# Hybrid layer with 32 experts: one set of 19 places for raw weights and their split parts, and a new order of experts

## The chip, the cores and the metric

The kernel runs on one core of one Trainium2 chip. The metric is the device time of one execution in microseconds; before the change it is 1484.7 us, the median of 3 runs (1482.25 to 1488.44).

## What is computed

512 tokens of 1024 numbers go through one layer: an input projection, four retention heads and eight sliding-window attention heads, an output projection `w_out` with a residual, then a mixture of 32 experts of which each token takes four, and last a gate with a small per-layer embedding and a final norm. The experts are nearly all of the weights:

```python
def expert_block(args):
    xblk, e = args
    h = xblk @ w_up[e] + b_up[e]
    return clamped_swiglu(h) @ w_down[e] + b_down[e]
```

`w_up[e]` is 1024 x 2048 and `w_down[e]` 1024 x 1024, both fp32: 12 MB for each expert.

## The kernel before

**Stages.** Stage 1 makes both kinds of heads, until about 227 us. The output projection, the router and the slot tables follow, until about 300 us; then the experts one after the other, until 1392 us; then the embedding gate and the norms.

**Pieces.** Weights arrive in pieces of 128 x 2048 fp32 (1 MB), eight for an expert's up products (`w_up_piece`) and four for its down products (`w_down_piece`). The list `pieces` holds their order: the four pieces of `w_out`, the eight up pieces of expert 0, and then for each expert the up pieces of the next one and the four down pieces of this one. `prefetch()` takes a place from the list `free`, issues the next piece's transfer on SP's queue (which works in order, a waiting transfer holds all behind it) and puts it on `queue`. Before the change `free` grows to 12 places, in three pools: three (`rawp`) from the start, five (`raw2`) once the memory of stage 1 is released, four (`raw3`) as the mixed heads are used up. At that release the kernel also makes `R.bias` from the down and up biases, on one of the raw places.

**Experts.** The string `BIG` says which experts get 128 rows ("L", 18 of 32) and which 64 ("S", 14). For an L expert each piece is split for three fp32r products: `split()` has ACT write `wh`, the rounded piece (L150), and DVE `wl`, what the rounding left out (L151). `wh` and `wl` have three rotating buffers each (`whp`, `wlp`). `up()` (L847) does for each up piece four products of `xTh` with `wh`, four of `xTl` with `wh`, four of `xTh` with `wl`; `down()` (L928) does for each down piece two groups of six in the same order, with two columns each. An S expert doesn't split its pieces; it uses each piece raw with pairs of products on 64 columns (L864, `up64` and `down64`). A piece is taken by `next_piece()` (split) or `whole_piece()` (raw); both put the raw place back on `free` and call `prefetch()`.

**Order of the work.** In the loop over e, `up` of expert e comes first, then its activation (`act`: `sg` on ACT, `a` on DVE), the transposes of the next expert's tokens (`prep`, L300, or `prep64`, L815), then `down` of expert e - 1 and the transposes of the activation (`act_t`). The tokens of expert e + 1 come by an indirect DMA (`xe`, L800), the results leave by another (`acc`, L942). In `w_out`'s section (L307 to L309 by `mm3`) PE takes three products per row block; the last transposes of `y` in stage 1 are on L598. The scores of the attention (L479) are products of 64 rows, of one or the other half.

Of the kernel before, what the change touches and what calls it, by code (L numbers as in the profile page):

```python
# [11 lines left out]
F32 = mybir.dt.float32  # L12
# [10 lines left out]
P = 128  # L23
# [13 lines left out]
RAW1, RAW2, RAW3 = 3, 5, 4  # L37
# [9 lines left out]
BIG = [c == "L" for c in "LL" + "SLSLSLSLSLSLSLL" + "SLSLSLSLSLSLLLS"]  # L47
# [48 lines left out]
def hymba_kernel(ctx, tc, x, p, positions, rel_bias_table, g_mix_norm, w_in, b_in, ret_norm_g,  # L96
# [27 lines left out]
    rawp = pool(ctx, "rawp", RAW1)  # L124
    whp = pool(ctx, "whp", 3)
    wlp = pool(ctx, "wlp", 3)
# [7 lines left out]
    R = SimpleNamespace(eid={})  # L134
    free = [rawp] * RAW1

    def raw_tile(dt=F32):
        pl_ = free.pop(0)
        return pl_.tile([P, 2048], dt, name="raw"), pl_

    def split(raw, parts=None, dst=None):
        if dst is None:
            wh = whp.tile([P, 2048], F32R, name="wh")
            wl = wlp.tile([P, 2048], F32R, name="wl")
        else:
            wh, wl = dst
# [51 lines left out]

    pieces = [w_ret(0, 0), w_ret(0, 4), w_kv, w_half(w_in, 0, 2048), w_half(w_in, 4, 2048)]
# [6 lines left out]
    for e in range(1, E + 1):  # L206
        if e < E:
            pieces += [w_up_piece(e, k) for k in range(8)]
        pieces += [w_down_piece(e - 1, f) for f in range(4)]
    n_moe = len(pieces)  # L210
# [6 lines left out]
    def prefetch(after=None):  # L217
        if free and state["next"] < min(len(pieces), state["limit"]):
            t, pl_ = raw_tile()
            if after is not None:  # L220
                nc.scalar.activation(t[:, 0:1], after[:, 0:1], AF.Copy)
            pieces[state["next"]](t)
            queue.append((t, pl_))
            state["next"] += 1

    def next_piece(parts=None, dst=None, more=True):
        t, pl_ = queue.pop(0)
        r = split(t, parts, dst)
        free.append(pl_)
# [3 lines left out]

    def whole_piece(use):

        t, pl_ = queue.pop(0)
        use(t)
        free.append(pl_)
# [88 lines left out]
    raw3 = pool(ctx, "raw3", RAW3)  # L327
    mix = [raw3.tile([P, 2048], F32R, name="raw").rearrange("p (a k t) -> a p k t", a=2, k=KD) for _ in range(NT)]
# [6 lines left out]
    p1 = px.enter_context(ExitStack())  # L335
    actp = pool(p1, "actp")
# [9 lines left out]
    prefetch()  # L346
    nc.sync.dma_start(out=xts[1], in_=x_v[:, 1, :])
    prefetch()
# [116 lines left out]
    def attention(nb):  # L465
# [8 lines left out]
        for gp in range(2):  # L474

            s_ps = [sps.tile([P, 512], F32, name="s_ps").rearrange("p (a b) -> p a b", a=2) for _ in range(2)]
            for g in range(2):
# [800 lines left out]
```

## Time and profile before

| | |
|---|---|
| median of 3 runs | 1484.7 us |
| the profiled execution's time | 1485.38 us |
| its span | 1483.6 us |
| PE busy | 1351.3 us (91%), 6090 instructions |
| DVE busy | 830.1 us (56%) |
| ACT busy | 677.7 us (46%) |
| moved by DMA | 462.47 MB, mean 312 GB/s |
| up and down pieces, from issue to landing | 17.4 and 17.9 us, median |

A row of the timeline gives the start in us, the length, the engine, the line, the operation and its output and inputs, the count, and in brackets the idle time of the engine before it and what ended it. PE's lengths are those of pipelined products, whose ends are modelled: their starts tell more. `SPq` is the issue of a transfer on SP's queue. PEclk is the granted clock of TensorE, 1.00 being full speed (2.4 GHz).

### The profile page before, as it was taken

Reading aid. Unit: us, or ns where it says so; the run is one execution under the profiler, and the core shown is the slowest. Engines: PE = TensorE matmul, PEld = TensorE weight load, DVE = VectorE, ACT = ScalarE, POOL = GpSimd, SP = SyncE. Lnnn points to the kernel's source line nnn. Section 1 sums busy time; section 2 is a strip of 40 time slices with the busy share of each in tenths; the row PEclk is TensorE's granted clock in tenths of the full one; section 3 lists DMA queues with packets and bytes.
Section 4 is the critical chain, followed back from the end, with each engine's and each line's share of the span. In section 5 each row is a group of like instructions: output and inputs, shape, how many; then the busy total and the mean of one; then the engine's idle time right before and its main releaser. Section 6 shows DMA issues by size and latency. Waiting matters only on the chain. (4 is left out here: it accounts for less than half of the span.)

```text
span 1483.6 us, 16861 instructions
## 1 busy us (share of the span) xinstructions
PE 1351.3 (91%) x6090; PEld 907.1 (61%) x6091; DVE 830.1 (56%) x1005; ACT 677.7 (46%) x750; POOL 224.4 (15%) x238
## 2 busy tenths in 40 slices
PE   5999999588999999999999999999999999999885
PEld 4777777466657474655647657465655647675564
DVE  6637774776547263544637647354553726683356
ACT  5333443455536253543626535343452625573443
POOL 2213241474100000000000000000100000000023
PEclk9999999788999999999999999999999999999998
DMA  9332046667899999999999999999999999987511
GB/s 272 118 109 58 29 142 254 237 254 280 318 402 396 403 405 396 406 399 393 392 396 408 393 388 387 375 403 396 386 394 399 395 387 400 391 328 283 183 72 43
DMA packets 110427, 462.47 MB, mean 312 GB/s; under 512 B 10830, under 2 KB 29180, under 8 KB 77568
## 3 DMA queue, kind: packets, MB, share of 16 engines
q1 hardware_dynamic: 99584, 436.24, 74.8%
q0 software_dynamic: 10320, 24.52, 6.5%
q8 instruction: 49, 0.80, 0.2%
q10 hardware_dynamic: 432, 0.57, 0.1%
q14 instruction: 42, 0.34, 0.1%
HBM read 447.26 MB, written 18.73 MB: 314 GB/s over the span
## 5 line engine op out<-in xcount | busy, mean ns | idle before, releaser
L151 DVE TENSOR_TENSOR wl<-raw,wh 128x2048 fp32r<-128x2048 f32 (+2 forms) x243 | 530.2, 2222 | 151.8 <-ACT wh L150 143.8
L150 ACT ACTIVATE wh<-raw 128x2048 fp32r<-128x2048 f32 (+2 forms) x243 | 442.9, 1858 | 110.2 <-PE up L847 52.2
L864 PE MATMUL up<-raw,xTh 128*64 128x512 f32 x896 | 195.3, 594 | 0.0
L896 DVE TENSOR_SCALAR a<-up 128x512 f32<-128x512 f32 x50 | 32.9, 687 | 267.8 <-ACT sg L895 267.8
L847 PE MATMUL up<-wh,xTh 128*128 128x512 f32 x576 | 162.8, 405 | 9.2 <-ACT wh L150 7.8
L895 ACT ACTIVATE sg<-up 128x512 f32<-128x512 f32 x50 | 27.9, 595 | 297.0 <-issue 158.5
L847 PE MATMUL up<-wl,xTh 128*128 128x512 f32 x576 | 160.9, 401 | 2.2 <-DVE wl L151 2.2
L847 PE MATMUL up<-wh,xTl 128*128 128x512 f32 x576 | 161.0, 401 | 1.4 <-DVE xTl L292 1.4
L864 PEld LDWEIGHTS up<-raw,xTh 128*64 128x64 f32 x896 | 63.1, 137 | 124.6 <-issue 120.0
L847 PEld LDWEIGHTS up<-wh,xTh 128*128 128x128 f32 x576 | 108.7, 191 | 40.5 <-ACT wh L150 13.1
L847 PEld LDWEIGHTS up<-wl,xTh 128*128 128x128 f32 x576 | 109.0, 191 | 32.8 <-DVE wl L151 7.0
L847 PEld LDWEIGHTS up<-wh,xTl 128*128 128x128 f32 x576 | 109.8, 191 | 28.2 <-DVE xTl L292 1.8
L928 PE MATMUL dn<-wh,aTh 128*128 128x512 f32 x288 | 100.8, 434 | 23.8 <-ACT wh L150 23.8
L928 PE MATMUL dn<-wl,aTh 128*128 128x512 f32 x288 | 104.0, 446 | 15.9 <-DVE wl L151 15.9
L942 POOL DMA_INDIRECT acc<-y,slot_i x30 | 45.4, 1514 | 443.3 <-ACT y L937 434.8
L800 POOL DMA_INDIRECT xe<-xg,slot_i x30 | 31.9, 1064 | 485.9 <-PE dn L857 261.0
L864 PE MATMUL dn<-raw,aT 128*64 128x512 f32 x448 | 102.9, 598 | 0.0
L928 PE MATMUL dn<-wh,aTl 128*128 128x512 f32 x288 | 98.2, 425 | 0.0
L928 PEld LDWEIGHTS dn<-wh,aTh 128*128 128x128 f32 x288 | 59.4, 211 | 42.8 <-ACT wh L150 27.3
L928 PEld LDWEIGHTS dn<-wl,aTh 128*128 128x128 f32 x288 | 58.5, 212 | 35.5 <-DVE wl L151 23.1
L914 DVE SCALAR_TENSOR_TENSOR aTl<-tp,aTh 128x512 fp32r<-128x512 f32 x36 | 24.1, 689 | 90.2 <-ACT aTh L913 90.2
L928 PEld LDWEIGHTS dn<-wh,aTl 128*128 128x128 f32 x288 | 59.3, 206 | 15.0
(340 smaller groups left out, 1571.9 us busy)
## 6 DMA issues: line engine op xcount, KB each, us to landing
raw<-in_w_up_dram SPq DMA_DIRECT2D x256, 1024.0 KB, 17.4
raw<-in_w_down_dram SPq DMA_DIRECT2D x128, 1024.0 KB, 17.9
raw<-in_w_in_dram SPq DMA_DIRECT2D x32, 256.0 KB, 4.8
raw<-in_w_out_dram SPq DMA_DIRECT2D x4, 1024.0 KB, 5.0
raw<-in_w_ple_gate_dram SPq DMA_DIRECT2D x4, 1024.0 KB, 10.4
raw<-in_w_in_dram SPq DMA_DIRECT2D x3, 1024.0 KB, 5.7
xt<-in_x_dram SPq DMA_DIRECT2D x4, 512.0 KB, 6.5
h<-in_x_dram POOLq DMA_DIRECT2D x4, 512.0 KB, 7.6
```

The source lines that it names most:

```text
L150: R.split_act = nc.scalar.activation(to(wh), src(raw), AF.Copy)
L151: R.split_dve = nc.vector.tensor_tensor(out=to(wl), in0=src(raw), in1=to(wh).bitcast(F32), op=ALU.subtract)
L800: return nc.gpsimd.indirect_dma_start(out=dst[0:n, 0:D // h], out_offset=None, in_=xg.rearrange("s (h d) -> (s h) d", h=h), in_offset=bass ...
L847: nc.tensor.matmul(h[n // 2][:, n % 2 * 512:n % 2 * 512 + 512], lhsT=a[:, k, :], rhs=w[:, n * 512:(n + 1) * 512], start=(k == 0 and a is x ...
L864: R.pair = nc.tensor.matmul(o[v * 64:v * 64 + 64, c:c + 512], lhsT=xT[:, k, :], rhs=w[:, v * n + c:v * n + c + 512], start=False, stop=las ...
L895: nc.scalar.activation(sg[:, cs], hv[:, :, 0], AF.Silu, scale=ALPHA)
L896: nc.vector.tensor_scalar(a[:, cs], hv[:, :, 1], LIMIT + 1.0, 1.0 - LIMIT, op0=ALU.min, op1=ALU.max)
L914: nc.vector.scalar_tensor_tensor(flat(l[:, g4, :]), in0=flat(t), scalar=1.0 / ALPHA, in1=flat(h[:, g4, :]).bitcast(F32), op0=ALU.mult, op1 ...
L928: m = nc.tensor.matmul(o[:, n * 512:(n + 1) * 512], lhsT=a[:, k, :], rhs=w[:, kk * 1024 + n * 512:kk * 1024 + (n + 1) * 512], start=False, ...
L942: nc.gpsimd.indirect_dma_start(out=acc.rearrange("s (h d) -> (s h) d", h=h), out_offset=bass.IndirectOffsetOnAxis(ap=idx[0:n, :], axis=0), ...
```

## The change

All raw pieces now have named places, 19 in the end: a0 to a2 from the start, b0 to b8 in place of the five of `raw2`, c0 to c3 of the mixed heads, h0 to h2, which were `whp`. The pool `wlp` lives in stage 1 only. Afterwards `split()` takes two places for `wh` and `wl` by `raw_tile(part=True)`; a second list `spare` holds places that parts have given back: parts take from `spare` first and raw pieces from `free` first, each from the other list if its own is empty. `used()`, called behind a piece's products, appends its two places to `spare`. `room()` tells `prefetch()` whether to hold back: among the next `depth` pieces to be used it counts those that will be split (the others are in `plain`) and wants two places for each, less the places that earlier ones give back.

Besides: the last 15 experts come in a new order, with as many L and S; `xn` of the router lies on two raw places; `sg` is half as wide, `y` has one buffer; for e = 1 the turn of the next expert's tokens (`turn()`) comes behind the down products of expert 0; the score products are pinned in alternation of the two halves; all four `w_out` pieces come in the new `prefetch()`, which loops by itself; the gains of the end lie in the place of the tile `last`.

The core of the diff:

```diff
@@ -34,7 +34,7 @@
 LIMIT = 7.0
 S_MAX = float(ALPHA * LIMIT / (1.0 + math.exp(-ALPHA * LIMIT)))
 CAP = 96
-RAW1, RAW2, RAW3 = 3, 5, 4
+RAW1, RAW2, RAW3 = 3, 9, 4
 FAR = 1000.0
...
@@ -44,7 +44,7 @@
-BIG = [c == "L" for c in "LL" + "SLSLSLSLSLSLSLL" + "SLSLSLSLSLSLLLS"]
+BIG = [c == "L" for c in "LL" + "SLSLSLSLSLSLSLL" + "SLSLSLLSLLSLLSS"]
 NBIG = sum(BIG)
 RANK = [sum(BIG[:t]) if BIG[t] else NBIG + t - sum(BIG[:t]) for t in range(len(BIG))]
 CAPS = 64
...
@@ -121,9 +121,8 @@
         return stack.enter_context(tc.tile_pool(name=name, bufs=bufs, reuse_waits="tile", **kw))
     const = pool(ctx, "const")
-    rawp = pool(ctx, "rawp", RAW1)
-    whp = pool(ctx, "whp", 3)
-    wlp = pool(ctx, "wlp", 3)
+    rawp = pool(ctx, "rawp")
+    whp = pool(ctx, "whp")
     small = pool(ctx, "small", 3)
     cst = const.tile([P, C_REV], F32, name="cst")
...
@@ -131,19 +130,28 @@
     ident = cst[:, C_ID:C_ID + P]
-    R = SimpleNamespace(eid={})
-    free = [rawp] * RAW1
-
-    def raw_tile(dt=F32):
-        pl_ = free.pop(0)
-        return pl_.tile([P, 2048], dt, name="raw"), pl_
+
+    R = SimpleNamespace(eid={}, wlp=None, depth=2)
+    held = []
+    free = [(rawp, f"a{j}") for j in range(RAW1)]
+    spare = []
+    high = [(whp, f"h{j}") for j in range(3)]
+
+    def raw_tile(dt=F32, name="raw", part=False):
+        first, other = (spare, free) if part else (free, spare)
+        place = (first or other).pop(0)
+        return place[0].tile([P, 2048], dt, name=name, tag=place[1], bufs=1), place
     def split(raw, parts=None, dst=None):
-        if dst is None:
-            wh = whp.tile([P, 2048], F32R, name="wh")
-            wl = wlp.tile([P, 2048], F32R, name="wl")
+        if dst is not None:
+            wh, wl = dst
+        elif R.wlp is not None:
+            high.append(high.pop(0))
+            wh = whp.tile([P, 2048], F32R, name="wh", tag=high[-1][1], bufs=1)
+            wl = R.wlp.tile([P, 2048], F32R, name="wl")
         else:
-            wh, wl = dst
+            (wh, p0), (wl, p1_) = raw_tile(F32R, "wh", True), raw_tile(F32R, "wl", True)
+            held.append((p0, p1_))
         if parts is None:
             parts = [(lambda t: t, lambda t: t)]
         for src, to in parts:
...
@@ -206,7 +215,11 @@
     for e in range(1, E + 1):
         if e < E:
             pieces += [w_up_piece(e, k) for k in range(8)]
+            if not BIG[e]:
+                plain.update(range(len(pieces) - 8, len(pieces)))
         pieces += [w_down_piece(e - 1, f) for f in range(4)]
+        if not BIG[e - 1]:
+            plain.update(range(len(pieces) - 4, len(pieces)))
     n_moe = len(pieces)
     pieces += [w_proj_piece]
     for c in range(2):
...
@@ -214,28 +227,43 @@
     queue = []
     state = {"next": 0, "limit": n_first}
-    def prefetch(after=None):
-        if free and state["next"] < min(len(pieces), state["limit"]):
-            t, pl_ = raw_tile()
+    def room():
+
+        n = len(free) + len(spare)
+        if R.wlp is not None:
+            return n > 0
+        c = state["next"] - len(queue)
+        ahead = [j not in plain for j in range(c, min(c + R.depth, len(pieces)))]
+        return n > 0 and n + 2 * len(held) > 2 * sum(ahead) - (ahead.index(True) if any(ahead) else 0)
+
+    def prefetch(after=None, n=99):
+        while n and state["next"] < min(len(pieces), state["limit"]) and room():
+            t, place = raw_tile()
             if after is not None:
                 nc.scalar.activation(t[:, 0:1], after[:, 0:1], AF.Copy)
             pieces[state["next"]](t)
-            queue.append((t, pl_))
+            queue.append((t, place))
             state["next"] += 1
-
-    def next_piece(parts=None, dst=None, more=True):
-        t, pl_ = queue.pop(0)
-        r = split(t, parts, dst)
-        free.append(pl_)
+            n -= 1
+
+    def next_piece(parts=None, more=True):
+
+        t, place = queue.pop(0)
+        r = split(t, parts)
+        free.append(place)
         if more:
             prefetch()
         return r
+    def used():
+        spare.extend(held.pop(0))
+        prefetch()
+
     def whole_piece(use):
-        t, pl_ = queue.pop(0)
+        t, place = queue.pop(0)
         use(t)
-        free.append(pl_)
+        free.append(place)
         prefetch()
...
@@ -474,10 +503,12 @@
         for gp in range(2):
             s_ps = [sps.tile([P, 512], F32, name="s_ps").rearrange("p (a b) -> p a b", a=2) for _ in range(2)]
+            m = None
             for g in range(2):
                 for kv, rows in enumerate(kvs):
-                    nc.tensor.matmul(s_ps[kv][:, g, 0:nk * P], lhsT=aqT[rows, gp * 2 + g, nb * P:(nb + 1) * P],
-                                     rhs=akT[rows, k0:k0 + nk * P], start=True, stop=True)
+                    with tc.issue_after(m.ins) if m is not None else nullcontext():
+                        m = nc.tensor.matmul(s_ps[kv][:, g, 0:nk * P], lhsT=aqT[rows, gp * 2 + g, nb * P:(nb + 1) * P],
+                                             rhs=akT[rows, k0:k0 + nk * P], start=True, stop=True)
             for kv, rows in enumerate(kvs):
                 h0 = kv * 4 + gp * 2
                 h2_ = slice(h0, h0 + 2)
...
@@ -613,9 +644,11 @@
     p1.close()
-    raw2 = pool(right, "raw2", RAW2, side="right")
+    R.wlp = None
+    raw2 = pool(right, "raw2", side="right")
     rt = pool(right, "rt", side="right")
-    free += [raw2] * RAW2
+    free += [(raw2, f"b{j}") for j in range(RAW2)]
+    free += high[1:]
...
@@ -627,16 +660,16 @@
     R.bias = rt.tile([P, 1536], F32R, name="bias")
     sv = b_raw[:, 0:1024].rearrange("p (c t) -> p c t", t=2)[:, :, 1]
     nc.gpsimd.tensor_scalar(sv, sv, 1.0, None, op0=ALU.add)
-    b_hi = whp.tile([P, 2048], F32R, name="wh")
+    b_hi = whp.tile([P, 2048], F32R, name="wh", tag=high[0][1], bufs=1)
     nc.scalar.activation(b_hi[:, 0:1536], b_raw[:, 0:1536], AF.Copy)
     for r0 in (0, 64):
         nc.gpsimd.memset(b_raw[r0:r0 + E, 0:1536], 0.0)
     nc.vector.scalar_tensor_tensor(R.bias, in0=b_hi[:, 0:1536].bitcast(F32), scalar=cst[:, C_SGN:C_SGN + 1],
                                    in1=b_raw[:, 0:1536], op0=ALU.mult, op1=ALU.add)
+    xns = [raw_tile(F32, "xn") for _ in range(2)]
     state["limit"] = n_moe
-    while free:
-        prefetch()
-    free.append(b_pool)
+    prefetch()
+    free += [b_pool, high[0]]
     prefetch()
     ident_b = const.tile([P, P], BF16, name="ident_b")
...
@@ -746,7 +779,7 @@
                 mm3(ps, (mix[i][0][:, k, :], mix[i][1][:, k, :]), [kslice(w, k % 4) for w in ws[k // 4]],
                     k == order[0], k == order[-1])
             if c == 1:
-                free.append(raw3)
+                free.append((raw3, f"c{i}"))
                 prefetch()
             nc.vector.tensor_tensor(out=h1[:, i, cs], in0=ps, in1=h1[:, i, cs], op=ALU.add)
             t = tp.tile([P, 4, P], F32, name="tp")
...
@@ -764,7 +797,7 @@
                 nc.vector.tensor_copy(out=lg[:, i, :], in_=o)
             else:
                 nc.vector.tensor_tensor(out=lg[:, i, :], in0=o, in1=lg[:, i, :], op=ALU.add)
-                xn = tl.tile([P, D], F32, name="xn")
+                xn = xns[i % 2][0][:, 0:D]
                 for cc in range(2):
                     cs = slice(cc * 512, (cc + 1) * 512)
                     nc.gpsimd.tensor_tensor(out=xn[:, cs], in0=h1[:, i, cs], in1=g_moe[:, cs], op=ALU.mult)
...
@@ -775,6 +808,11 @@
                 nc.sync.dma_start(out=xg[tok, :], in_=xn)
                 nc.sync.dma_start(out=acc[tok, :], in_=h1[:, i, :])
                 route_tile(i, logits)
+        used()
+        used()
+    free += [t[1] for t in xns]
+    R.depth = 2
+    prefetch()
     def route(posm_ap, v_ap):
...
@@ -846,6 +884,7 @@
                 for n in range(4):
                     nc.tensor.matmul(h[n // 2][:, n % 2 * 512:n % 2 * 512 + 512], lhsT=a[:, k, :],
                                      rhs=w[:, n * 512:(n + 1) * 512], start=(k == 0 and a is xT[0] and w is wh), stop=False)
+            used()
         R.up_end = add_bias(h, e, 0, 1024, start=False, stop=True)
         return h
...
@@ -928,12 +967,13 @@
                         m = nc.tensor.matmul(o[:, n * 512:(n + 1) * 512], lhsT=a[:, k, :],
                                              rhs=w[:, kk * 1024 + n * 512:kk * 1024 + (n + 1) * 512],
                                              start=False, stop=(k == KD - 1 and w is wl))
+            used()
             if f == 1:
                 R.dn_mid = m
         return o
     def gated(o, gate):
-        y = R.sb.tile([P, D], F32, name="y")
+        y = R.sb.tile([P, D], F32, name="y", bufs=1)
         nc.scalar.activation(y[:, 0:o.shape[1]], o, AF.Copy, scale=gate)
         return y
...
@@ -887,14 +926,14 @@
     def act(h):
-        sg = R.sb.tile([P, FF], F32, name="sg", bufs=1)
         a = R.sb.tile([P, FF], F32, name="a", bufs=1)
         for v, h_ in enumerate(h):
             hv = h_.rearrange("p (c t) -> p c t", t=2)
             cs = slice(v * 512, (v + 1) * 512)
-            nc.scalar.activation(sg[:, cs], hv[:, :, 0], AF.Silu, scale=ALPHA)
+            sg = R.sb.tile([P, 512], F32, name="sg", bufs=1)
+            nc.scalar.activation(sg, hv[:, :, 0], AF.Silu, scale=ALPHA)
             nc.vector.tensor_scalar(a[:, cs], hv[:, :, 1], LIMIT + 1.0, 1.0 - LIMIT, op0=ALU.min, op1=ALU.max)
-            R.act = nc.vector.scalar_tensor_tensor(a[:, cs], in0=sg[:, cs], scalar=S_MAX, in1=a[:, cs], op0=ALU.min,
+            R.act = nc.vector.scalar_tensor_tensor(a[:, cs], in0=sg, scalar=S_MAX, in1=a[:, cs], op0=ALU.min,
                                                    op1=ALU.mult)
         return a
...
@@ -1044,6 +1084,7 @@
     open_pools(mx, "moe")
     with tc.issue_after(R.last.ins), tc.issue_after(R.last_act.ins):
+        R.depth = 3
         ahead = [next_piece() for _ in range(2)]
         with tc.issue_after(R.split_dve.ins):
             xT = prep(xe[0])
...
@@ -1066,9 +1107,12 @@
             if e == 0:
                 read_slots()
                 static_gather(2)
-            if e + 1 < E:
+            def turn():
+                return (prep if BIG[e + 1] else prep64)(xe[(e + 1) % 2])
+
+            if e + 1 < E and e != 1:
                 with tc.issue_after(R.up_end.ins):
-                    xT = (prep if BIG[e + 1] else prep64)(xe[(e + 1) % 2])
+                    xT = turn()
         if e == E - 1:
             last = raw_tile()
...
@@ -1091,6 +1135,8 @@
         if e < E - 1:
             with tc.issue_after(R.dn_mid.ins) if e else nullcontext():
                 aT = act_t(a) if BIG[e] else act_t64(a)
+        if e == 1:
+            xT = turn()
     h2 = [t for _ in range(2) for t in raw_tile()[0].rearrange("p (a n) -> a p n", a=2)]
     proj = [t for _ in range(2) for t in raw_tile()[0].rearrange("p (a n) -> a p n", a=2)]
...
@@ -1178,10 +1223,11 @@
     with tc.issue_after(ld.ins):
         for _ in range(2):
             prefetch()
-    g_ple = bcast(ep2, g_ple_norm[0], D, "g_ple", nc.sync)
-    g_fin = bcast(ep2, g_final, D, "g_fin", nc.sync)
+    g_ple, g_fin = last[0][:, 0:D], last[0][:, D:2 * D]
+    for dst, src in ((g_ple, g_ple_norm[0]), (g_fin, g_final)):
+        nc.sync.dma_start(out=dst, in_=src.rearrange("(o n) -> o n", o=1).broadcast_to([P, D]))
     ws = [ws]
-    free += [t[1] for t in (last, tmp, tf, tr)]
+    free += [t[1] for t in (tmp, tf, tr)]
     hT = {}
     ss1 = {}
```

The order of the instructions moves in three places that matter below.

ACT, at a pair of experts (`wh` are the splits, `sg` an activation, `xTh` and `aT64` transposed tokens and activations, `y` a result); the number behind a name is that of its buffer, and a wait on a PE semaphore is one for products. Before:

```order
L150 ACTIVATE wh_3777<-raw_3634 128x2048 [waits DMAHW4_49]
L150 ACTIVATE wh_3795<-raw_3640 128x2048 [waits DMAHW5_49]
L150 ACTIVATE wh_3813<-raw_3646 128x2048 [waits DMAHW6_49,DVE_49,PE_49]
L150 ACTIVATE wh_3848<-raw_3681 128x2048 [waits DMAHW7_49,DVE_49,PE_49]
L150 ACTIVATE wh_3876<-raw_3697 128x2048 [waits DMAHW0_49,DVE_49,PE_49]
```

With the change:

```order
L158 ACTIVATE wh_3781<-raw_3558 128x2048 [waits DMAHW3_49,DMAHW1_49,PE_49]
L934 ACTIVATE sg_3758<-up_3698 128x512 [waits DVE_49,PE_49,Activation_49]
L319 ACTIVATE xTh_3762<-tp_3764 128x512 [waits PE_49]
L319 ACTIVATE xTh_3762<-tp_3771 128x512 [waits PE_49]
L158 ACTIVATE wh_3797<-raw_3576 128x2048 [waits DMAHW4_49,DVE_49,PE_49]
L158 ACTIVATE wh_3813<-raw_3578 128x2048 [waits DMAHW5_49,DVE_49,PE_49]
L854 ACTIVATE aT64_3850<-tp_3851 128x4x2x64 [waits PE_49]
L158 ACTIVATE wh_3829<-raw_3580 128x2048 [waits DMAHW6_49,DVE_49,PE_49]
```

The first down split has moved ahead of the S expert's activation, and every split waits for products.

SP's queue, around the `w_out` pieces (behind the last pieces of stage 1). Before:

```order
L170 DMA raw<-in_w_in_dram 128x4x128 x24
L156 DMA raw<-in_w_out_dram 128x4x512 x2
L186 DMA raw<-in_w_up_dram 128x2048 x3
L156 DMA raw<-in_w_out_dram 128x4x512 x2
L186 DMA raw<-in_w_up_dram 128x2048 x6
```

With the change:

```order
L178 DMA raw<-in_w_in_dram 128x4x128 x24
L194 DMA raw<-in_w_up_dram 128x2048
L164 DMA raw<-in_w_out_dram 128x4x512 x4
L194 DMA raw<-in_w_up_dram 128x2048 x9
```

All four `w_out` pieces now stand behind a first up piece.

PE at the end of stage 1 (`mm` and `s_ps` are sums in PSUM; L307 to L309, now L335 to L337, are `w_out`'s products). Before:

```order
L315 MATMUL mm<-wl,act_h 128x512 x4
L307 MATMUL mm<-wh,raw 128x512
L308 MATMUL mm<-wh,raw 128x512
L309 MATMUL mm<-wl,raw 128x512
L307 MATMUL mm<-wh,raw 128x512
```

With the change:

```order
L606 MATMUL or_ps<-vs,sc 128x128
L608 MATMUL or_ps<-r_prev,qkT 128x128
L629 MATMUL tp<-cst,y 128x128 x2
L335 MATMUL mm<-wh,raw 128x512
L336 MATMUL mm<-wh,raw 128x512
```

The first of `w_out`'s products came right behind the last input projection, with the last retention products and the transposes of `y` among those that followed; now it comes behind both.

## Rows read from the trace of the kernel before

**Rows 1.** Busy by stretch: length, PE, PEld, DVE, ACT, POOL, granted clock, DMA share, GB/s.

```profile
302.00:400.00 98.00, 89.63 (x384) 63.57 (x385) 63.19 (x45) 50.86 (x38) 48.42 (x34) 0.93 0.76 280
400.00:1300.00 900.00, 853.03 (x3711) 535.30 (x3709) 472.75 (x309) 415.20 (x345) 68.78 (x53) 0.96 1.01 395
```

**Rows 2.** Timeline of PE, two pairs' starts: start us, length, engine, line, operation, count.

```profile
905.32 1.10 PE L847 MATMUL up<-wh,xTh 128*128 128x512 f32 x4
...
1237.51 1.10 PE L847 MATMUL up<-wh,xTh 128*128 128x512 f32 x4
```

**Rows 3.** The splits' own lines: count, then ns at least, median, at most.

```profile
L150 ACT ACTIVATE wh<-raw x243: 613/1914/1944, 14.9 to 1419.0; 128x2048 fp32r<-128x2048 f32 x116, 128x512 fp32r<-128x512 f32 x4, 128x1024 fp32r<-128x1024 f32 x2
L151 DVE TENSOR_TENSOR wl<-raw,wh x243: 673/2286/2825, 18.2 to 1420.9; 128x2048 fp32r<-128x2048 f32 x116, 128x512 fp32r<-128x512 f32 x4, 128x1024 fp32r<-128x1024 f32 x2
```

**Rows 4.** Timeline of expert 1's up products.

```profile
336.30 1.09 PE L847 MATMUL up<-wh,xTl 128*128 128x512 f32 x4
...
337.23 1.09 PE L847 MATMUL up<-wl,xTh 128*128 128x512 f32 x4
337.43 1.92 ACT L150 ACTIVATE wh<-raw 128x2048 fp32r<-128x2048 f32 x1 [1.02 <-PE up L847]
```

**Rows 5.** Timeline of a 64-row expert's end and the down products behind it.

```profile
1061.86 0.73 PE L834 MATMUL up<-bias,sel 64*128 64x512 f32 x4
...
1086.03 1.09 PE L300 MATMUL tp<-cst,xe 128*128 128x128 f32 x8
...
1087.05 0.49 PE L834 MATMUL dn<-bias,sel 64*128 64x512 f32 x2
...
1087.75 5.51 ACT L150 ACTIVATE wh<-raw 128x2048 fp32r<-128x2048 f32 x3
...
1089.69 6.69 DVE L151 TENSOR_TENSOR wl<-raw,wh 128x2048 fp32r<-128x2048 f32 x3 [0.39 <-ACT wh L150]
...
1089.71 0.73 PE L928 MATMUL dn<-wh,aTh 128*128 128x512 f32 x2 [2.17 <-ACT wh L150]
...
1092.04 0.94 PE L928 MATMUL dn<-wl,aTh 128*128 128x512 f32 x2 [1.12 <-DVE wl L151]
...
1104.38 1.10 PE L847 MATMUL up<-wh,xTh 128*128 128x512 f32 x4
```

**Rows 6.** Timeline of PE: down products behind a 128-row expert, start and end.

```profile
856.84 0.73 PE L834 MATMUL up<-bias,sel 64*128 64x512 f32 x4
...
871.90 1.51 PE L864 MATMUL up<-raw,xTh 128*64 128x512 f32 x6
```

**Rows 7.** Busy by stretch, around the start of down products (columns as in rows 1).

```profile
1089.71:1092.40 2.69, 1.56 (x6) 0.99 (x7) 2.69 (x2) 2.69 (x2) 0.00 (x0) 1.00 1.04 411
1092.40:1095.80 3.40, 3.40 (x10) 2.63 (x9) 3.40 (x2) 1.94 (x2) 0.00 (x0) 0.50 1.01 313
```

**Rows 8.** SP's queue and PE around w_out; last, L307's products alone in a stretch.

```profile
203.79 10.01 SPq L186 DMA_DIRECT2D raw<-in_w_up_dram  x3
217.78 9.97 SPq L156 DMA_DIRECT2D raw<-in_w_out_dram  x2
...
227.43 0.41 PE L598 MATMUL tp<-cst,y 128*128 128x128 f32 x2 [1.04 <-DVE y L595]
...
212.70:227.45 14.75, 5.79 (x14) 2.45 (x13) 1.00 0.83 299
```

**Rows 9.** Timeline of PE after expert 1's up products.

```profile
355.05 0.73 PE L834 MATMUL up<-bias,sel 64*128 64x512 f32 x4
361.33 1.09 PE L815 MATMUL tp<-cst,xe 128*128 128x128 f32 x4 [5.55 <-DMA xe<-xg,slot_i]
```

**Rows 10.** Score products: two runs of them, and all of them in a stretch.

```profile
145.84 0.70 PE L479 MATMUL s_ps<-akT,aqT 64*128 64x256 f32 x2
...
183.17 1.34 PE L479 MATMUL s_ps<-akT,aqT 64*128 64x256 f32 x8
...
85.00:190.00 105.00, 14.23 (x64) 8.24 (x64) 1.00 0.18 51
```

More of the change, by code (lines that the diff above doesn't have):

```diff
@@ L197, in w_proj_piece @@
                           in_=w_ple_proj.rearrange("(k p) c -> p k c", p=P))
+    plain = set()
     pieces = [w_ret(0, 0), w_ret(0, 4), w_kv, w_half(w_in, 0, 2048), w_half(w_in, 4, 2048)]
@@ L326, in hymba_kernel @@
     right = ctx.enter_context(ExitStack())
-    raw3 = pool(ctx, "raw3", RAW3)
-    mix = [raw3.tile([P, 2048], F32R, name="raw").rearrange("p (a k t) -> a p k t", a=2, k=KD) for _ in range(NT)]
+    raw3 = pool(ctx, "raw3")
+    mix = [raw3.tile([P, 2048], F32R, name="raw", tag=f"c{j}", bufs=1).rearrange("p (a k t) -> a p k t", a=2, k=KD) for j in range(NT)]
     mm = pool(px, "mm", 2, PSUM)
@@ L335, in hymba_kernel @@
     p1 = px.enter_context(ExitStack())
+    R.wlp = pool(p1, "wlp", 3)
     actp = pool(p1, "actp")
@@ L345, in hymba_kernel @@
     g_mix = bcast(n1, g_mix_norm[0], D, "g_mix", nc.sync)
-    prefetch()
+    prefetch(n=1)
     nc.sync.dma_start(out=xts[1], in_=x_v[:, 1, :])
-    prefetch()
+    prefetch(n=1)
     for i in range(2, NT):
@@ L635, in hymba_kernel @@
                                    in1=b_raw[:, 0:1536], op0=ALU.mult, op1=ALU.add)
+    xns = [raw_tile(F32, "xn") for _ in range(2)]
     state["limit"] = n_moe
-    while free:
-        prefetch()
-    free.append(b_pool)
+    prefetch()
+    free += [b_pool, high[0]]
     prefetch()
@@ L1016, in read_slots @@
     def read_slots():
-        tab = R.sb.tile([P, D], F32, name="y")[0:CAP, 0:8 * E].rearrange("p (k f) -> p k f", k=4)
-        half = R.sb.tile([P, D], F32, name="y")[:, 0:E]
+        tab = R.sb.tile([P, D], F32, name="y", bufs=1)[0:CAP, 0:8 * E].rearrange("p (k f) -> p k f", k=4)
+        half = R.sb.tile([P, KD, 64], F32, name="aT64", bufs=1)[:, 0, 0:E]
         for k in range(4):
@@ L1126, in hymba_kernel @@
             nc.gpsimd.dma_start(out=gate_d.rearrange("e p i -> p e i")[:, :, i], in_=gates[:, i, :])
-        pe = ov.tile([P, NT], F32, name="pe")
-        ge = ov.tile([P, NT], F32, name="ge")
+        pe, ge = t_f[:, 1024:1024 + NT], t_f[:, 1032:1032 + NT]
         with tc.For_i(0, E, 1) as ev:
@@ L1141, in hymba_kernel @@
                 idx, gate = route(pe.rearrange("p (i o) -> p i o", o=1), v)
-                xd = R.sb.tile([P, D], F32, name="y")
+                xd = R.sb.tile([P, D], F32, name="xd", bufs=1)
                 nc.gpsimd.memset(xd, 0.0)
@@ L1235, in hymba_kernel @@
     project(mm.tile([P, D], F32, name="dn"), (3,))
-    ws.append([next_piece(), next_piece(dst=(raw_tile(F32R)[0], raw_tile(F32R)[0]))])
+    used()
+    ws.append([next_piece() for _ in range(2)])
     gate(0, 0)
```

## The prediction

> **What bounds the kernel now.** I read the busy times by stage first, then the weight splits, then the timeline of one pair of experts. From 400 to 1300 us the DMA engines are busy for the whole stretch, moving 395 GB/s, and TensorE for 853 of 900 us [rows 1]: weights arrive about as fast as products use them. Five pairs of a 64-row and a 128-row expert last from 905.32 to 1237.51, so 66.4 us each [rows 2]; a pair brings 24 pieces of 1 MB, one every 2.77 us.
>
> A 128-row expert needs each piece split, ACT writing `wh` (1914 ns median) and DVE `wl` (2286 ns) [rows 3], and the split of the next piece runs during the products of this one. The reader should see that in the first expert's successor: ACT starts a `wh` at 337.43, 0.20 us after PE has turned from the `xTl` products to the `wl` products at 337.23, and PE doesn't wait [rows 4]. Four products take 337.23 - 336.30 = 0.93 us, 0.2335 each, so a piece's twelve take 2.80. That works because `wh` and `wl` have three buffers each: this ACT instruction overwrites the `wh` of two or three pieces ago.
>
> **The places after the change.** Parts now come from the same 19 places as raw pieces. `raw_tile(part=True)` takes from `spare` if there is anything, else from `free`; `used()` puts both places of a piece back on `spare`. For the first two experts three pieces are split ahead, `spare` grows to six places, and the pairs rotate as before. Then comes expert 2, which is plain. While all pieces in sight are plain, `room()` asks for nothing to be held back, and raw pieces take `free` and then `spare` until both are empty. The next split piece finds `spare` empty and takes two places from `free`; its `used()` returns just these two; the piece after it finds two in `spare` and takes the same two, though `room()` has kept some four more in `free`. From the down pieces of expert 1 on every split piece overwrites the pair of the piece before it. The ACT rows of the order agree: of the splits at a pair's down pieces, before, the first two wait for a transfer alone; now each one also waits for PE.
>
> **The chain that this makes.** Its edges are in the rows. After the last product that reads `wh`, ACT starts 0.20 us later [rows 4]; 1.92 us of split (337.43 plus its duration); from ACT's end to PE's start 0.12 us (1087.75 + 5.51/3 = 1089.59, PE 1089.71); `wl` follows `wh` on DVE with 0.10 us or less and takes 2.23 (6.69/3), and PE starts 0.12 after it (1089.69 + 2.23 = 1091.92, PE 1092.04) [rows 5].
> - An up piece: eight products read `wh` (1.87), then 0.20 + 1.92 + 0.12, so **4.11 us** from start to start in place of 2.80. The piece's `wl` is ready at about 2.31 and its last products end at 3.24, within this time. Eight pieces: 7 x 4.11 + 3.24 = 32.0 us.
> - A down piece takes its products in two groups of six, and the second group's `wh` products stand behind the first group's `wl` products. 0.93 us of `wh`, a wait for `wl` until 2.31, 0.47, then 0.93 of `wh`: last use at 3.71, plus 2.24: **5.95 us** in place of 2.80.
> - Down pieces behind a 64-row expert: now 18.35 us, from 1086.03 to 1104.38. The transposes and the bias take the first 1.5 (1087.05 + 0.49 - 1086.03) [rows 5]. The first piece's split runs beside the 64-row products, its `wl` until about 2.7; the second piece starts at 6.3, the third at 12.2, the fourth at 18.2, the next up at 24.1.
> - Down pieces behind a 128-row expert: now 871.90 - 856.84 = 15.06 us [rows 6]; 23.2 by the same steps, with a little less ahead of the first piece.
>
> **The sum**, against the profiled execution: it took 1485.38 us, its span is 1483.6, and it lies 0.7 above the median of 1484.7.
> - Up: the pair's 66.4 less its 64-row part (1061.86 to 1086.03, 24.17) less its down part (18.35) leaves 23.9; 32.0 - 23.9 = 8.1, for 16 experts (18 less the first two): **+130**.
> - Down, from expert 3 on, 16 experts: now 13 behind a 64-row expert and 3 behind a 128-row one, 13 x 18.35 + 3 x 15.06 = 283.7; the new string has 12 and 4, 12 x 24.1 + 4 x 23.2 = 382.0: +98. Expert 1's down products, 15.06 to 24.1: +9. Together **+107**.
> - Clock. TensorE's granted clock falls in short episodes: after a stretch in which PE was busy for 1.56 of 2.69 us (58%) it was 0.50, the 1.2 GHz level, for the next 3.40 [rows 7]. In the down chain PE is busy 2.80 of 5.95 us, 47%; in the up chain 2.80 of 4.11, 68%. At the low level a down piece needs 1.87 (past that `wl` waits to 2.31) + 0.93 + 1.87 + 2.24 = 7.35, 1.4 more. Bounds: none, or 68 pieces x 1.4 = 95. I take half of the pieces: **+48**.
> - Front. Now two `w_out` pieces were asked for in stage 1, and PE does their products from 212.72 to 227.45, beside the last transposes of `y` (227.43): 14 of the first kind [rows 8], some 41 of the three. In the change all four `w_out` stand on SP behind a `w_up` piece, the kind that waits for places of the new pool (203.79 before), and PE's `w_out` products stand behind the last `y` transposes. So 41 x 0.2335 = 9.6 us of work moves behind 227.4, and the split of a piece (1.92 + 2.29 less what overlaps) comes ahead of it: **+15** (5 to 20).
> - The first down products no longer wait for the gathered rows of expert 2: PE is idle 5.55 us ahead of 361.33 [rows 9]: **-5** (0 to -8, if the restart at the low clock goes too).
> - Score products: 64 of them, 14.23 us busy; eight in a row take 1.34, 0.168 each, two in a row 0.70 [rows 10]. If the pinned order makes all as cheap as the run of eight, 64 x 0.168 = 10.7, less 3.5; PE has other work between them, so **-2** (0 to -3.5). The Trainium skill, TensorEngine Tiling (Array Packing), section Theoretical Speedup, lets products of up to 64 rows run up to twice as fast, as two tiles of the array; by it this term would be -7, and the trace agrees with part of that only.
> - The smaller `sg`, one `y`, the gains kept in the raw place: each a wait of below 1 us beside work that is now waiting anyway; nothing.
>
> 130 + 107 + 48 + 15 - 5 - 2 = 293; 1485 + 293 = **1778 us**. Deeper prefetch gains nothing here: pieces arrive every 2.77 us and are used every 4.11 or 5.95. The other way round, the transfers will run into full places.
>
> **Rivals.**
> - *The clock stays up.* Same chain, no low-clock episodes: 1778 - 48 = 1730. For it: at 68% nothing may happen, and the chain is regular. Against: [rows 7]. It lies in my range.
> - *The clock falls in the up chain too.* An up piece is then 8 x 0.467 + 2.24 = 5.98, +1.87 for 128 pieces, 239: about 2015. Against: at the low level PE would be busy 94% of the time, and the rows show the clock coming back under full load; 4 in 100.
> - *The parts rotate* (the other side; the change would then do what its places allow). If `spare` holds six places or more in each 128-row expert, the chain isn't there, 19 places let the queue run further ahead, and the transfers decide. DMA was busy 0.76 of 98 us before 400 [rows 1], so 23.5 us could be won there and no more; with the -5 and -2 inside that, 1485 - 24 = about 1461. It decides as soon as a split finds other places than its predecessor's. Against: the bookkeeping above, and each split's wait for PE. 3 in 100. The Trainium skill, DMA: Bandwidth & Descriptors, section Specifications, gives 358 GB/s as a core's share of HBM and 435 as the fabric's ceiling: the trace's 395 is above the first, and by the second a pair's transfers could come down to some 60 us (an estimate from that page); the nearest row has 411 [rows 7].
> - *Only part of the splits are chained* (every second expert finds other places): half of 237 + 48, so about 1635. Against: `spare` is emptied at each plain expert and filled with two. 5 in 100.
>
> **How the numbers follow.** My forecast with the clock anywhere between its bounds: 0.88; clock low in the up chain 0.04; half chained 0.05; rotating 0.03. The range takes the forecast's own bounds: clock 0 to 95, front 5 to 20, edges of 0.1 us on some 190 pieces (20): 1700 to 1845. A difference under about 0.5% can't be told from none. Faster 0.03, same 0.01, slower 0.96.
>
> **What would show it.** Right: PE's busy share from 400 to 1300 down to some 70%, waits of PE for ACT's `wh` of about 1.3 us at nearly each up piece, of ACT's `wh` for PE at nearly each piece, DMA share near 0.8, up stretches of 32 us and down stretches of 23 to 26, w_out products starting at about 232. Wrong: a pair that still takes 66 us, or ACT starting a `wh` while PE still reads the one before it.

## Result: 1762.16 us, 1.186 times the time before

The changed kernel takes 1762.16 us (median of 4 runs, 1754.96 to 1767.12), the kernel before 1485.3 beside it (1482.25 to 1488.44); the ratio is 1.186, its 95% interval 1.181 to 1.191. The forecast was 1778 with a range of 1700 to 1845. The span of the profiled run is 1762.4 us, 278.8 more than before.

The stretches that answer to [rows 1], with the same columns (the experts' stretch is now 250 us longer; the last line is the end of the kernel, 91.2 us long before):

```profile
320.00:420.00 100.00, 90.86 (x382) 61.66 (x380) 58.25 (x39) 47.59 (x37) 42.77 (x32) 0.94 0.92 342
420.00:1570.00 1150.00, 940.64 (x3714) 528.55 (x3714) 506.45 (x324) 440.45 (x354) 102.33 (x53) 0.96 0.82 302
...
1671.00:1762.00 91.00, 65.48 (x295) 52.14 (x293) 47.74 (x107) 35.60 (x65) 22.11 (x18) 0.89 0.22 78
```

DMA's share falls from 1.01 to 0.82, TensorE's from 95% to 82%; the granted clock is the same 0.96. TensorE and the DMA engines are both idle for more of the time than before. The list of waits says for what (engine and line that waits, what it waits for, us in total, times, longest):

```profile
DVE wl L159 <- ACT wh L158: 627.7, 213, 17.3
...
ACT wh L158 <- PE dn L967: 252.5, 60, 5.3
ACT wh L158 <- DVE wl L159: 242.4, 101, 2.4
...
PE up L885 <- ACT wh L158: 106.0, 124, 1.5
...
PEld dn L967 <- ACT wh L158: 68.8, 47, 2.0
PEld dn L967 <- DVE wl L159: 66.8, 54, 1.6
```

ACT, DVE and PE stand in a ring: PE waits for `wh`, DVE waits for `wh`, and ACT waits for whoever read the last `wh`. In the up products of expert 5 the ring looks like this on the timeline; what answers in the kernel before is [rows 4], where PE had no wait. In this timeline and the next the rows of weight loads (PEld) and of SP are left out:

```profile
521.38 2.29 DVE L159 TENSOR_TENSOR wl<-raw,wh 128x2048 fp32r<-128x2048 f32 x1 [2.03 <-ACT wh L158]
521.39 1.20 PE L885 MATMUL up<-wh,xTh 128*128 128x512 f32 x4 [0.79 <-ACT wh L158]
522.43 1.09 PE L885 MATMUL up<-wh,xTl 128*128 128x512 f32 x4
523.72 1.20 PE L885 MATMUL up<-wl,xTh 128*128 128x512 f32 x4 [0.19 <-DVE wl L159]
523.75 1.91 ACT L158 ACTIVATE wh<-raw 128x2048 fp32r<-128x2048 f32 x1 [2.41 <-DVE wl L159]
525.70 2.29 DVE L159 TENSOR_TENSOR wl<-raw,wh 128x2048 fp32r<-128x2048 f32 x1 [2.03 <-ACT wh L158]
525.72 1.21 PE L885 MATMUL up<-wh,xTh 128*128 128x512 f32 x4 [0.79 <-ACT wh L158]
```

One turn takes 525.72 - 521.39 = 4.33 us in place of 2.80. The bracket to look at is the one that ends ACT's wait. It doesn't name PE, which had read `wh` for the last time by 523.4. It names DVE, which reads `wh` too when it makes `wl`, until 523.67. So the turn is a `wh` and a `wl` one behind the other, 1.91 + 2.29 + 0.13 us between them.

The down products, where [rows 5] and [rows 7] stood before:

```profile
508.22 1.91 ACT L158 ACTIVATE wh<-raw 128x2048 fp32r<-128x2048 f32 x1 [3.60 <-PE dn L967]
510.16 2.29 DVE L159 TENSOR_TENSOR wl<-raw,wh 128x2048 fp32r<-128x2048 f32 x1 [3.70 <-ACT wh L158]
510.18 0.74 PE L967 MATMUL dn<-wh,aTh 128*128 128x512 f32 x2 [1.53 <-ACT wh L158]
510.76 0.63 PE L967 MATMUL dn<-wh,aTl 128*128 128x512 f32 x2
512.51 0.86 PE L967 MATMUL dn<-wl,aTh 128*128 128x512 f32 x2 [1.12 <-DVE wl L159]
```

```profile
510.18:512.51 2.33, 1.21 (x4) 0.68 (x5) 2.27 (x1) 0.00 (x0) 0.00 (x0) 1.00 0.33 130
512.51:515.90 3.39, 3.39 (x8) 2.17 (x8) 0.00 (x0) 0.79 (x1) 0.00 (x0) 0.56 0.69 225
517.07:551.43 34.36, 27.27 (x100) 17.09 (x100) 18.32 (x8) 14.35 (x8) 2.37 (x1) 1.00 0.68 227
```

The piece before started at 504.19, so a down piece takes 5.99 us. The three stretches (columns as above) show the clock's part: after the wait for `wl` it is 0.56 for 3.39 us; through the up products with their short gaps it stays at 1.00.

### The profile page after: what moved, and what is told of

Its sections match the earlier page's. It is cut to its first block, busy times and chain, and to the rows that moved or that the text cites. A ratio compares the mean times of both kernels' runs of the same rounds, so it can differ in the third digit from the quotient of the medians.

```text
span 1762.4 us, 16933 instructions
## 1 busy us (share of the span) xinstructions
PE 1452.8 (82%) x6090; PEld 888.1 (50%) x6091; DVE 840.8 (48%) x1003; ACT 690.1 (39%) x754; POOL 255.3 (14%) x238
## 5 line engine op out<-in xcount | busy, mean ns | idle before, releaser
L159 DVE TENSOR_TENSOR wl<-raw,wh 128x2048 fp32r<-128x2048 f32 (+2 forms) x244 | 542.8, 2226 | 651.4 <-ACT wh L158 627.7
L158 ACT ACTIVATE wh<-raw 128x2048 fp32r<-128x2048 f32 (+2 forms) x244 | 452.2, 1856 | 686.0 <-PE dn L967 252.5
L885 PE MATMUL up<-wh,xTh 128*128 128x512 f32 x576 | 175.3, 426 | 107.3 <-ACT wh L158 106.0
L903 PE MATMUL up<-raw,xTh 128*64 128x512 f32 x896 | 208.1, 601 | 0.7 <-ACT xTh L854 0.7
L885 PE MATMUL up<-wl,xTh 128*128 128x512 f32 x576 | 172.3, 421 | 24.0 <-DVE wl L159 24.0
L967 PE MATMUL dn<-wl,aTh 128*128 128x512 f32 x288 | 113.3, 479 | 43.0 <-DVE wl L159 42.6
L885 PEld LDWEIGHTS up<-wl,xTh 128*128 128x128 f32 x576 | 100.0, 191 | 92.8 <-DVE wl L159 77.7
L838 POOL DMA_INDIRECT xe<-xg,slot_i x30 | 50.7, 1689 | 619.7 <-PE dn L896 353.0
L982 POOL DMA_INDIRECT acc<-y,slot_i x30 | 60.9, 2029 | 528.0 <-ACT y L977 507.5
L903 PEld LDWEIGHTS dn<-raw,aT 128*64 128x64 f32 x448 | 31.3, 137 | 59.7 <-issue 59.7
```

Of the source, the lines that this page charges most:

```text
L158: R.split_act = nc.scalar.activation(to(wh), src(raw), AF.Copy)
L159: R.split_dve = nc.vector.tensor_tensor(out=to(wl), in0=src(raw), in1=to(wh).bitcast(F32), op=ALU.subtract)
L838: return nc.gpsimd.indirect_dma_start(out=dst[0:n, 0:D // h], out_offset=None, in_=xg.rearrange("s (h d) -> (s h) d", h=h), in_offset=bass ...
L885: nc.tensor.matmul(h[n // 2][:, n % 2 * 512:n % 2 * 512 + 512], lhsT=a[:, k, :], rhs=w[:, n * 512:(n + 1) * 512], start=(k == 0 and a is x ...
L903: R.pair = nc.tensor.matmul(o[v * 64:v * 64 + 64, c:c + 512], lhsT=xT[:, k, :], rhs=w[:, v * n + c:v * n + c + 512], start=False, stop=las ...
L967: m = nc.tensor.matmul(o[:, n * 512:(n + 1) * 512], lhsT=a[:, k, :], rhs=w[:, kk * 1024 + n * 512:kk * 1024 + (n + 1) * 512], start=False, ...
```

## Experiments

**One pair in the kernel before.** `wh` and `wl` keep their own pools, but from expert 2 on each use the same buffer again:

```diff
+    def place(i, few):
+        if not (R.one and few):
+            turns[i] = (turns[i] + 1) % 3
+        return f"{i}{turns[i]}"
...
-            wh = whp.tile([P, 2048], F32R, name="wh")
-            wl = wlp.tile([P, 2048], F32R, name="wl")
+            wh = whp.tile([P, 2048], F32R, name="wh", tag=place(0, True), bufs=1)
+            wl = wlp.tile([P, 2048], F32R, name="wl", tag=place(1, True), bufs=1)
```

> The kernel before, with one buffer of wh and one of wl from expert 2 on, nothing else changed. If the chain alone explains the loss: up stretches of 33 to 34 us in place of 23.5 (16 of them, +165) and +80 to +115 on the down stretches: 1730 to 1770 us. If the chain needs the change's other parts: below 1600.

Measured: 1770.98 us (one run), its up stretches 33.6 to 35.2 us long. A single pair, without any other part of the change, costs as much as the whole change: the ring alone is enough. The upper edge of the expectation was missed by 1 us.

**One buffer of `wl` alone.** As above, with `place(0, False)` for `wh`.

> The kernel before, with one buffer of wl from expert 2 on and three of wh. Then DVE waits for the last product of the piece before: 0.93 + 0.20 + 2.29 + 0.12 = 3.54 us for an up piece, up stretches of about 28 us, a down piece 1.87 + 0.20 + 2.29 + 0.12 = 4.48; about 1485 + 72 + 75 = 1630 us. If only the wh place matters (ACT's wait): below 1510.

Measured: 1633.39 us (one run), up stretches of 26.7 to 30.0 us. On the page's groups of the two runs (busy, mean ns, idle before and its releaser), PE waits for the part that is short; the first fence is the run with one pair, the second the one with one `wl`:

```profile
L853 PE MATMUL up<-wh,xTh 128*128 128x512 f32 x576 | 175.0, 426 | 108.5 <-ACT wh L156 107.6
...
L853 PE MATMUL up<-wl,xTh 128*128 128x512 f32 x576 | 171.3, 419 | 24.0 <-DVE wl L157 24.0
```

```profile
L853 PE MATMUL up<-wl,xTh 128*128 128x512 f32 x576 | 173.9, 424 | 92.7 <-DVE wl L157 92.6
...
L853 PE MATMUL up<-wh,xTh 128*128 128x512 f32 x576 | 163.8, 407 | 1.3 <-ACT xTh L297 0.8
```

Here the sum of edges from the trace, with DVE's wait in it, came within 4 us of the 1633.

**Three pairs and two pairs in the change.** One line, with 5 (three pairs) or 3 (two):

```diff
-        first, other = (spare, free) if part else (free, spare)
+        first, other = (spare, free) if part and len(spare) >= 5 else (free, spare)
```

> The change, with parts taken from spare only when it holds five places or more (else from free), so that three pairs rotate. If the single pair is the loss: up stretches of 128-row experts back from 33.8 us to about 23.5, pairs from 83.5 to about 66, and a time of 1485 to 1515 us (the later start of the first expert, 16 us, stays). If the loss comes from room() holding raw pieces back or from the new order of experts: above 1650 us.

> The same with a threshold of three, so that two pairs rotate. By the chain ACT 1.92 and DVE 2.29 us for each piece are then both hidden under 2.80 us of products, so within 15 us of three pairs. If what counts is how many places parts have in proportion: half way, about 1620 us.

Measured: 1569.11 us with three pairs (ratio 1.055, 1.0525 to 1.0575) and 1537.45 with two (one run). The ring is gone: with three pairs the wait of PE's up products for ACT's `wh` falls from 106.0 to 37.8 us in all, and with two an up stretch is 24.1 to 25.8 us long. But 50 to 85 us above the kernel before are left, and three pairs are worse than two. Neither expectation held. Where the time may go shows in the stretch of the experts and on SP's queue (start, length, issue, count), with three pairs:

```profile
420.00:1380.00 960.00, 866.77 (x3701) 537.98 (x3700) 500.72 (x323) 437.02 (x354) 80.27 (x53) 0.97 0.93 360
```

```profile
739.19 6.80 SPq L200 DMA_DIRECT2D raw<-in_w_down_dram  x3
747.33 26.48 SPq L194 DMA_DIRECT2D raw<-in_w_up_dram  x4
```

Four pieces in 26 us, and a DMA share of 0.93: this fits `room()` holding raw pieces back for the parts, which the next run tests. Why three pairs lose more than two was not tried.

**Two separate stocks.** 13 places that only raw pieces take and six that only parts take:

```diff
-    free += [(raw2, f"b{j}") for j in range(RAW2)]
-    free += high[1:]
+    free += [(raw2, f"b{j}") for j in range(6)]
+    spare += high[1:] + [(raw2, f"b{j}") for j in range(6, RAW2)]
...
-        n = len(free) + len(spare)
...
+        return len(free) > 0
...
-    free += [b_pool, high[0]]
+    free.append(b_pool)
+    spare.append(high[0])
```

> The change with two separate stocks: 13 places that only raw pieces take and six that only parts take; room() asks only for a free raw place. If three pairs still lost 84 us because reserved places hold transfers back (gaps of up to 17 us on SP's queue, DMA share 0.93), pairs come back to 66.4 us and DMA to about 1.00: 1485 to 1505 us, the first expert still 16 us late. If the loss of three pairs lay in the order of experts or of the splits: above 1540.

Measured: 1498.36 us, ratio 1.01 (1.0067 to 1.0133), as in the first case of the expectation. SP's queue at the same place, and the stretch of 900 us:

```profile
743.21 19.78 SPq L194 DMA_DIRECT2D raw<-in_w_up_dram  x8
```

```profile
420.00:1320.00 900.00, 852.17 (x3747) 545.76 (x3746) 503.72 (x326) 438.48 (x357) 68.50 (x53) 0.98 1.01 392
```

Eight pieces in 20 us, DMA at 1.01 again as in [rows 1]. So the change's loss in the experts has two causes by its stock: one pair for parts (1762 to 1569 when it is three), and a common stock that holds transfers back (1569 to 1498 when it is two). The two don't add up to the price of each alone: one pair alone cost 284 us in the kernel before (1486.6 beside it), about as much as the whole change costs, so it seems that while the ring binds, the held-back transfers cost nothing more.

**The order of the experts alone**, in the kernel before (the new string in `BIG`):

> The kernel before with only the new string of experts. Transfers bind there, and the string moves as many L and S: within 6 us of 1485. If the two 64-row experts at the end cost their products in the open (a pair of S behind the last transfer): 1490 to 1500.

Measured: 1488.92 us, ratio 1.0027 (1.0008 to 1.0046), 4 us above 1484.9 beside it. It is inside the first expectation, 1 us short of the second; the experts end at 1396.7 us, with two 64-row experts' down products, 19.9 us, behind one another at the end. A small loss, not a gain.

**The front.** First the change itself, with `xn` on late places, so that two `w_out` pieces are asked for in stage 1 again:

```diff
-    xns = [raw_tile(F32, "xn") for _ in range(2)]
+    xns = []
+    for _ in range(2):
+        pl_ = free.pop()
+        xns.append((pl_[0].tile([P, 2048], F32, name="xn", tag=pl_[1], bufs=1), pl_))
```

> The change itself with only that order of places for xn. By my term for the front the first w_out products start before 215 us, the first expert product at about 300, and since the chain binds behind it, the end comes 12 to 20 us sooner: 1742 to 1750. If the late w_out is covered by the routing: unchanged, 1755 to 1767.

Measured: 1763.85 us (one run), no gain. Then the same edit on the two separate stocks:

> The same, and the router's xn takes places of the new pool, so that two w_out pieces get places of stage 1 and are asked for before the up piece. First expert product at about 300 us in place of 315; if the experts' time hangs on when their transfers start, the whole 10 to 16 us come back: 1472 to 1490. If transfers bind and start no earlier, within 5 us of the run above.

Measured: 1488.56 us (1.0031, 1.0013 to 1.0049), 9.8 below the run without the edit. The first expert's first product came at 320.2 us in the change with this edit (315.3 without), and at 304.5 in two stocks with it (318.6 without). The same transfers came early in both runs with the edit, but only in the second were they used early. On the timeline, the change first:

```profile
218.72 0.66 PE L629 MATMUL tp<-cst,y 128*128 128x128 f32 x2 [7.07 <-DVE y L626]
...
229.74 0.66 PE L629 MATMUL tp<-cst,y 128*128 128x128 f32 x2 [4.38 <-DVE y L626]
233.20 0.80 PE L335 MATMUL mm<-wh,raw 128*128 128x512 f32 x1 [2.80 <-ACT wh L158]
```

the change with early `w_out`:

```profile
127.40 42.44 SPq L164 DMA_DIRECT2D raw<-in_w_out_dram  x2
...
232.53 0.80 PE L335 MATMUL mm<-wh,raw 128*128 128x512 f32 x1 [2.17 <-ACT wh L158]
```

and two stocks with early `w_out`, where the first two parts lie on places that don't wait for stage 1's memory:

```profile
206.92 1.91 ACT L158 ACTIVATE wh<-raw 128x2048 fp32r<-128x2048 f32 x1
...
211.77 0.40 PE L330 MATMUL mm<-wh,raw 128*128 128x512 f32 x1
```

In the change PE idles 7.07 and 4.38 us in front of the transposes of `y`, with `w_out`'s products standing behind them; before, those products filled such gaps [rows 8]. The two runs differ in the stocks, so in where the parts lie and in `room()`; the transfers' time is excluded as the cause, and that it is the parts' places is an argument from the code, not a test by itself.

**Versions that might beat both.** Two stocks with the old string, the four earliest places given to the parts, the bias and `xn` on late places; 13 raw places and six for parts, or 15 and four:

```diff
-    free += [(raw2, f"b{j}") for j in range(RAW2)]
-    free += high[1:]
+    spare += [free.pop(0)] + high + [(raw2, f"b{j}") for j in range(7, RAW2)]
+    free += [(raw2, f"b{j}") for j in range(7)]
...
-    b_raw, b_pool = raw_tile()
+    b_raw, b_pool = late(F32, "raw")
```

> Two separate stocks of 13 raw places and six for parts, old order of experts, and the four earliest places of stage 1's pools given to the parts of the first two w_out pieces, the bias and xn on places of the new pool. If the first expert starts late because the parts of w_out lie over stage 1's memory (and not because its transfers come late), w_out's second split comes near 210 us in place of 232 and the first expert product at about 300; with one raw place more than before and transfers that bind: 1477 to 1487 us.

> The same with 15 raw places and four for parts (two pairs), and no third split ahead of the first expert. If the lead of the transfers decides, two more raw places give 2 x 2.77 us: 1471 to 1483. If two pairs make the chain felt (down pieces of 3 us and more): 1490 to 1520.

Measured: **1471.23 us** with 13 and six, ratio 0.991 (0.9889 to 0.9931), faster than both kernels and below what was expected; the split that should have come near 210 came at 232.96. With 15 and four 1488.45 (1.0022, 1.0003 to 1.004), between the two cases of its expectation. The first expert's first product came at 298.6 with 13 and at 307.5 with 15, and the stretch from 300 to 400 tells them apart, for 13 and then for 15 (before it was [rows 1], DMA 0.76):

```profile
300.00:400.00 100.00, 96.81 (x431) 68.74 (x430) 69.87 (x45) 59.03 (x44) 45.32 (x31) 0.98 0.87 318
```

```profile
300.00:400.00 100.00, 85.19 (x350) 58.94 (x352) 55.67 (x36) 46.35 (x35) 33.73 (x32) 0.88 0.69 250
```

With 13, the first experts run on nearly without a stop and DMA moves more in this stretch, where it still has room; afterwards, from 400 to 1300, it runs at 1.01 in both. That places come free sooner there is a reading of these rows; no run shows it alone. Whether 15 and four start late for the missing third split or for having two pairs was not tried.

**Single parts on the best version.** The transposes of expert 2's tokens put back ahead of the down products, and the new string:

> The version with 13 raw places and six for parts, with the transposes of expert 2's tokens back ahead of the first down products. If the move is worth what PE idled there before (5.55 us, 8 with the clock), and the four down pieces it releases let transfers go on: 1476 to 1481 us, 5 to 9 slower than with the move. If expert 2's products wait for their weights anyway: the same, 1469 to 1473.

> The version with 13 raw places and six for parts, with the change's new string of experts. By the run of the kernel before with the new string (4 us above before, its experts ending at 1396.7 in place of 1392.4, with two 64-row experts' down products in one piece at the end): 1474 to 1478. If the string's worth depends on the places: at or below 1471.

Measured: 1476.53 us (0.9947, 0.9926 to 0.9969) without the move and 1477.9 (0.9948, 0.9931 to 0.9965) with the new string, both as in the first case of their expectation, some 5 and 7 us above 1471.23. Against the kernel before, the interval of the first overlaps that of the best version and the other's touches it, so differences of this size are at the edge of what can be told. In the run without the move PE has this wait, where the version with it has none above 1.4 us:

```profile
356.88 1.09 PE L852 MATMUL tp<-cst,xe 128*128 128x128 f32 x4 [10.47 <-DMA xe<-xg,slot_i]
```

## Why the prediction was right, and where its steps failed

The mechanism was right: parts took the same pair again and again. It is shown from both sides, by the single pair put into the kernel before (1771) and by the ring's end with more pairs. By its own terms, from the starts and ends of each expert's products in both traces (down products from the last product ahead of them to the first behind them; where 64-row products stand between them, 13.95 us of theirs are taken off):

| term | forecast | measured |
|---|---|---|
| up products, 16 experts | +130 | +166.7 |
| down products and their clock | +155 | +106.5 |
| the 64-row experts' own products and the gaps beside them | 0 | -7.8 |
| front, with the score products | +13 | +16.2 |
| first experts (the moved transposes) | -5 | -3.6 |
| rest | 0 | +0.8 |
| sum | +293 | +278.8 |

- **Up.** The step "after the last product that reads `wh`, ACT starts 0.20 us later" left out a reader. DVE reads `wh` as well, until 2.3 us after PE's start, so a turn is 4.32 us and not 4.11, and an up stretch 33.8 us and not 32.0.
- **Down.** A piece took 5.99 us against 5.95 worked out, and a stretch behind a 64-row expert from its last product to the next up 25.4 to 27.9 us (11 of them mean 26.2; 27.9 for expert 1, which took 13.0 before and not the 15.06 of the sum) against 24.1 + 2.8. The clock's term was about right there if all above 24.1 is the clock's, 2.1 us for 2.8: the stretches with a clock of 0.77 to 0.80 are the long ones (26.8 to 27.9). What failed is the 23.2 us behind a 128-row expert, where the chain was taken to stand alone. The order there now puts the products of the 64-row expert between the pieces:

```profile
1017.57 0.62 PE L967 MATMUL dn<-wh,aTl 128*128 128x512 f32 x2
...
1019.05 1.93 PE L903 MATMUL up<-raw,xTh 128*64 128x512 f32 x6
1020.91 0.73 PE L967 MATMUL dn<-wh,aTh 128*128 128x512 f32 x2
1021.48 0.62 PE L967 MATMUL dn<-wh,aTl 128*128 128x512 f32 x2
1022.03 1.94 PE L903 MATMUL up<-raw,xTh 128*64 128x512 f32 x8
```

  From the end of up at 1013.4 to the end of both at 1045.1 are 31.7 us, at a granted clock of 1.00. The 64-row products take 13.95 of them where they stand alone (476.70 to 490.65), so 17.8 are left for the down products. That is nearer to the 15.06 of [rows 6] than to 23.2 + 2.8: while the chain waits, PE does the other expert's products, an overlap that the sum didn't have. Four such places, and the last 128-row expert, whose down products stand between those of the last 64-row expert (16.8 in place of 24.1 + 2.8), make some 43 us.
- **The total.** Up came out 37 us above its term and down 48 below. That the sum is only 14 off, and the time well within the range, is in part luck. The -7.8 of the 64-row experts was in no term, and its cause stays open.
- **Front.** The size was right (+15 against +16.2 for the first expert's first product, 299.1 to 315.3). The cause given, four `w_out` pieces behind a waiting up piece, was only half of it: with the pieces early the `w_out` products started 0.7 us sooner in the change (233.20 to 232.53).
- **Score products.** 64 of them are busy for 13.1 us against 14.2 in [rows 10]. The Trainium skill, TensorEngine Tiling (Array Packing), section Theoretical Speedup, states up to 2x for a small dimension of 64 or less; by it, at best, 7 us would have gone (an estimate from that page). The trace shows 1.1 us gone, 8% of the 14.2.
- **Hidden prefetch.** "The other way round, the transfers will run into full places" held: DMA 0.82. TensorE's share from 420 on was 82% where "some 70%" was named; the records' lengths fill part of the gaps (four products are shown 1.09 us long where they take 0.93 from start to start, [rows 4]). For the same reason PE's wait for `wh` shows as 0.79 us where about 1.3 was named.

Of the rivals, the clock never fell for long in the up products (14 of 16 stretches at 1.00, two at 0.93 and 0.94), the parts didn't rotate, and none of the 16 up stretches escaped the chain (33.6 to 35.2 us each).

## What to carry to other kernels

When buffers are joined into one stock with a preference ("take back what parts gave back first"), follow the list by hand through the first stretch in which nobody needs the preferred kind: what was lent out there doesn't come back, and the preference then hands out the same few places for good. Count every reader of a buffer when you work out when it comes free, the engine that makes the second part from the first among them. And a common stock with a reserve may cost more than fixed stocks: here 13 and six beat 19 in common with three pairs by some 70 us. Where a place's memory is still in use by an earlier stage, what is put there may start late; the front's runs point to that but don't test it alone.

## What the runs showed of the hardware

In the up chain PE had gaps of 0.79 and 0.19 us in each 4.32, and the granted clock stayed at 1.00 in 14 of 16 stretches; in the down chain, with gaps of 1.53 and 1.12 us in each 5.99, it was 0.77 to 0.93 on the mean of a stretch, with 0.56 in the 3.39 us behind one such pair of gaps. So the products of the up chain kept the 2.4 GHz level, and those of the down chain lost it for part of the time. The down chain has more idle time as well as longer gaps; which of the two counts, no run here shows.

Over 900 us one core moved 392 (two stocks) to 395 GB/s [rows 1] at a DMA share of 1.01.
